# First expert block's gating before the fourth scored block, v split in two around the gating, decay chain first in the mixer

## The chip, the cores and the metric

The kernel runs on one core of a Trainium2 chip. The metric is the device time of one execution in microseconds. TensorE (PE) multiplies and loads its weights on a second track (PEld), VectorE (DVE) and ScalarE (ACT) work element by element, GpSimd (POOL) gathers rows and starts some transfers, SyncE (SP) starts most transfers.

## The reference

One decoder layer over 512 tokens of width 1024, all in float32: an adaLN-modulated norm, one input projection that feeds a gated MLP and a gated delta rule with a short causal convolution, an output projection, then a retrieval layer over 128 x 128 = 16,384 single-neuron experts and a last norm. What matters here:

```python
q, k, v = silu(short_conv(p[q, k, v columns], conv_w))          # 4 taps along the tokens
g = -exp(a_log) * softplus(a + dt_bias); beta = sigmoid(b)        # decay of the delta rule
# retrieval: each token has 8 heads x 16 experts (ids) with softmax gates
act = gelu(einsum('pd,phkd->phk', hb, expert_u[ib]))
out = einsum('phk,phkd->pd', gb * act, expert_v[ib])
```

## The kernel before

Float32 products are made of three matmuls (lines 78 to 80): each operand is split into a high part, rounded by a copy (ACT as a rule), and a low part, the difference (`split_lo`, line 83, DVE as a rule); the products high x high, low x high and high x low are added up. So each block of weights needs an ACT copy and, after it, a DVE subtraction before its second matmul.

The stages, by the trace: modulation sums and first norm (0 to 53 us), the mixer (53 to about 340), output projection and the second norm, queries and top-16 routing (to 575), the gates written out dense and 47 of the 128 expert blocks scored early (to 733), the expert stage (733 to 1590), the end (to 1624).

**Mixer.** PE's order is written by hand: `ORD` lists projections (`k2`, `q3`), lengths (`l0` to `l3`, the squared norms of k and q by head), `d` (the decay matrices) and `f` (filling matmuls of v). Where the other engines' instructions stand is decided by a scheduler, by priorities; `tc.high_priority(n)` moves what is written inside it ahead by n places in that ranking. `conv_silu` (line 189) makes one 128 x 512 tile of the convolution: ACT copies the projection `pp` from PSUM to `xp` (line 195), DVE multiplies it by the first tap (196) and adds three shifted ones (198), ACT applies silu (199). The decay chain (lines 361 to 375) is some 20 tiny DVE operations on 128 x 16 with one exponential on ACT; it ends in `g`, and `beta` is a sigmoid. `pg` (line 420) is the first matmul that needs `g`; `pks` (385) are the transposes of k and q; `py` (524) are matmuls of the triangular solve, whose input `ms` DVE makes. Behind it DVE also makes modulation sums that are needed later (`wada`, line 208).

**Expert stage.** All engines run in the order of the program here. Three tiles of 128 tokens are dense (TD = 384): for each block of 128 experts the scores `pS` are 24 matmuls of 128x384 (lines 829 to 849), for the 81 blocks that were not scored early; the values `acc` are 18 matmuls of 128x512. The fourth tile of tokens goes by rows gathered for each of 128 picks: two DVE operations each (lines 1077, 1087). In `before(n)` and after it, iteration n makes what later iterations need:

- `split_v(n + 1)`: copy `vhi` on ACT (1137), difference `vlo` on DVE.
- `load_v(n + 3)`, `load_a(n + 3)`: transfers on SP; for an early block `sgr`, its stored scores; for every eighth block also the gates of eight blocks (1.5 MB, line 1116).
- the picks that are due, then `gated(n + 2)`: `a` = scores x gates on DVE (1122), its copy `ahi` on ACT (1124), `alo` on DVE.
- PE: values of block n, then scores of block n + 4, for which `split_u` has made `uhi` (ACT, 829) and `ulo` (DVE).

Before the loop, four blocks are scored (line 1202), then `split_v(0)` and `gated(0)`, `gated(1)` stand. The values of the last three blocks (125 to 127) are computed tile by tile, and `finish(t)` (line 1153) applies the last norm to each of the three dense tiles: line 1175 is its last multiplication by halves.

Of the kernel before, what the change touches and what calls it, by code (L numbers as in the profile page):

```python
# [59 lines left out]
def layer(ctx: ExitStack, tc: tile.TileContext, I, out):  # L60
# [88 lines left out]
    with ExitStack() as mixer:  # L149
# [42 lines left out]
        def conv_silu(c, dst, tmp, w=None, place=stream):  # L192
            def done(pp):
                xp, acc = tmp(), tmp()
                nc.scalar.copy(xp, pp)
                nc.vector.tensor_scalar(acc, xp, convw[:, c, 3:4], None, op0=OP.mult)
                for j in range(1, 4):
                    nc.vector.scalar_tensor_tensor(acc[:, j:], xp[:, :S - j], convw[:, c, 3 - j:4 - j], acc[:, j:], op0=OP.mult, op1=OP.add)
                nc.scalar.activation(dst, acc, AF.Silu)

            return project(w or I["w_in_t"][c], *hs, done, place)
# [111 lines left out]
        with ExitStack() as gdn, tc.manual_schedule(engines={nc.tensor.engine}):  # L313
# [47 lines left out]
            nc.vector.tensor_tensor(ga, ab[:, :, 0:H], bc(dtb[:, None, :], [P, NT, H]), op=OP.add)  # L361
            nc.vector.scalar_tensor_tensor(e, ga, -1.0, ga, op0=OP.mult, op1=OP.max)
            nc.scalar.activation(e, e, AF.Exp, scale=-1.0)
            nc.vector.tensor_scalar(s1, e, 2.0, None, op0=OP.add)
            nc.vector.reciprocal(s1, s1)
            nc.vector.tensor_tensor(s1, s1, e, op=OP.mult)
            nc.vector.tensor_tensor(s2, s1, s1, op=OP.mult)
            nc.vector.tensor_scalar(po, s2, 2.0 / 17, 2.0 / 15, op0=OP.mult, op1=OP.add)
            for q in (13, 11, 9, 7, 5, 3, 1):
                nc.vector.tensor_tensor(po, po, s2, op=OP.mult)  # L370
                nc.vector.tensor_scalar(po, po, 2.0 / q, None, op0=OP.add)
            nc.vector.tensor_tensor(po, po, s1, op=OP.mult)
            nc.vector.scalar_tensor_tensor(ga, ga, 0.0, po, op0=OP.max, op1=OP.add)
            g, beta, nbe = gcol("g"), gcol("beta"), gcol("nbe")
            nc.vector.tensor_tensor(g, ga, bc(nega[:, None, :], [P, NT, H]), op=OP.mult)
            nc.scalar.activation(beta, ab[:, :, H:2 * H], AF.Sigmoid)
# [678 lines left out]
    with ExitStack() as experts, tc.manual_schedule():  # L1055
# [48 lines left out]
        def load_a(b, place=None):  # L1104
            if kinds[b]:
                sgl = place or ap_.tile([P, TD], F32, tag="sgr", name="sgr", bufs=3)
                nc.sync.dma_start(sgl, sgd[early.index(b)])
                ready["s", b] = sgl
# [8 lines left out]
        def gated(b):  # L1117
# [6 lines left out]
            nc.scalar.copy(ahi, a)  # L1124
            alo = ap_.tile([P, TD], F32R, tag="alo", name="alo", bufs=LAST + 1)
# [8 lines left out]
        def split_v(b):  # L1134
            raw = ready.pop(("v", b))
            hi = vp.tile([P, D], F32R, tag="vhi", name="vhi", bufs=LAST)
            nc.scalar.copy(hi, raw)  # L1137
            lo = vp.tile([P, D], F32R, tag="vlo", name="vlo", bufs=LAST)
            split_lo(nc.vector, lo, raw, hi)
            ready["vs", b] = hi, lo  # L1140
# [12 lines left out]
        def finish(t, ff, eng):  # L1153
# [17 lines left out]
            for i, cs in enumerate(halves):  # L1171
                if i:
                    nc.scalar.mul(x2[:, cs], y[:, cs], rs[:, 0:1])
                else:
                    nc.vector.tensor_scalar(x2[:, cs], y[:, cs], rs[:, 0:1], None, op0=OP.mult)
# [12 lines left out]
        for i in range(3):  # L1188
            load_a(i)
# [12 lines left out]
        for b in range(LEAD):  # L1202
            score_ahead(b, b < LEAD - 1)
        split_v(0)
        for b in range(2):
            gated(b)
# [4 lines left out]
        def before(n):  # L1211

            if n + 1 < NK:
                split_v(n + 1)
            if n + 3 < NK and n + 3 not in aside:
                load_v(n + 3)
                load_a(n + 3)

        picked_tile = finish(NDT, [facc[:, :512], facc[:, 512:]], nc.gpsimd)
        for n in range(NK - LAST):  # L1220
# [14 lines left out]
            gated(n + 2)  # L1235
# [7 lines left out]
        for n in range(NK - LAST, NK - 1):  # L1243
            before(n)
            if n + 2 < NK:
                gated(n + 2)
# [53 lines left out]
```

## Time and profile before

| | us |
|---|---|
| median of 3 runs | 1622.62 (1621.18 to 1624.57) |
| the profiled execution | 1626.11 |
| its span, first to last instruction | 1624.4 |
| PE / PEld / DVE / ACT / POOL busy | 1551.5 / 1370.3 / 1298.5 / 637.4 / 479.9 |
| mean granted clock of PE | 0.981 of full speed |

The profile is of one execution. A matmul's shown duration overlaps the next one's, so that the distance between two starts is what it costs; in the timelines the bracket behind a row is the idle time of that engine just before it and what ended it.

### The profile page before, as it was taken

The numbers are of one execution on the slowest core, as the hardware profiler recorded it, in microseconds if no ns is written. First come the engines' busy times: TensorE is split into PE (matmuls) and PEld (weight loads), VectorE is DVE, ScalarE is ACT, GpSimd is POOL, SyncE is SP. The second block draws the span as 40 slices with busy tenths as digits, with TensorE's granted clock in tenths as the row PEclk, the third lists the DMA queues.
The fourth block names the chain that finished last, engine by engine and source line by source line (L and its number), as shares of the span: only waits on it lengthen the run. The fifth ranks groups of instructions, "written<-read, shape, count | busy, mean of one in ns | idle before, by whom it ended". The sixth has DMA issues, their size and how long they took to land.

```text
span 1624.4 us, 22848 instructions
## 1 busy us (share of the span) xinstructions
PE 1551.5 (96%) x8499; PEld 1370.3 (84%) x8499; DVE 1298.5 (80%) x2470; ACT 637.4 (39%) x939; POOL 479.9 (30%) x362
## 2 busy tenths in 40 slices
PE   6889999999998989999999999999999999999996
PEld 5678988887897979998888888888888888888884
DVE  6999845556999999974688888887888888888766
ACT  4542224344345545653333333333333333333334
POOL 0000000005436600001244444444444454544210
PEclk9989999999999999999999999999999999999998
DMA  9343511354214567777899999999899999999872
GB/s 373 123 162 103 188 53 56 107 173 133 79 59 128 164 229 290 280 268 251 299 329 342 347 360 314 341 355 335 312 350 368 347 320 338 340 339 322 301 243 98
DMA packets 135086, 402.80 MB, mean 248 GB/s; under 512 B 12480, under 2 KB 50752, under 8 KB 133312
## 3 DMA queue, kind: packets, MB, share of 16 engines
q1 hardware_dynamic: 96800, 262.41, 46.5%
q0 software_dynamic: 38176, 138.95, 23.2%
q8 instruction: 66, 1.08, 0.3%
q14 instruction: 44, 0.36, 0.1%
HBM read 362.71 MB, written 38.60 MB: 247 GB/s over the span
## 4 chain that ended last, share of the span: by engine, by line
PE 67%; DVE 17%; DMA 6%; issue 5%; ACT 4%; SPq 0%; POOL 0%; DVEq 0%; ACTq 0%
PE pS L78 8%; PE acc L78 8%; PE acc L79 8%; PE acc L80 8%; PE pS L80 8%; PE pS L79 7%; DMA uraw<-in_u_t 3%; PE pp L78 3%; PE pp L79 3%; PE pp L80 3%; DMA wada<-in_w_ada_c 2%; PE pq L79 2%; PE pq L80 2%; PE pq L78 2%; DVE wada L208 2%
## 5 line engine op out<-in xcount | busy, mean ns | idle before, releaser
L1070 POOL DMA_INDIRECT u_rows<-in_u_rows,rows x128 | 205.2, 1603 | 554.2 <-DVE dots L1077 338.0
L78 PE MATMUL pS<-hhi,uhi 128*128 128x384 f32 x1024 | 354.7, 346 | 1.4 <-ACT uhi L829 1.4
L80 PE MATMUL pS<-hhi,ulo 128*128 128x384 f32 x1024 | 347.0, 339 | 9.4 <-POOL ulo L83 7.5
L79 PE MATMUL pS<-hlo,uhi 128*128 128x384 f32 x1024 | 345.6, 337 | 0.0
L78 PE MATMUL acc<-vhi,ahi 128*128 128x512 f32 x768 | 302.7, 394 | 6.3 <-ACT ahi L1124 3.8
L79 PE MATMUL acc<-vlo,ahi 128*128 128x512 f32 x768 | 301.6, 393 | 2.3 <-DVE vlo L83 2.3
L80 PE MATMUL acc<-vhi,alo 128*128 128x512 f32 x768 | 300.8, 392 | 0.0
L1124 ACT CAST ahi<-a 128x384 fp32r<-128x384 f32 x128 | 65.7, 513 | 480.6 <-DVE a L1122 480.6
L80 PEld LDWEIGHTS pS<-hhi,ulo 128*128 128x128 f32 x1024 | 193.9, 189 | 12.2 <-POOL ulo L83 8.8
L78 PEld LDWEIGHTS pS<-hhi,uhi 128*128 128x128 f32 x1024 | 194.0, 189 | 5.4 <-ACT uhi L829 2.5
L83 DVE TENSOR_TENSOR vlo<-vraw,vhi 128x1024 fp32r<-128x1024 f32 x126 | 154.4, 1225 | 54.0 <-ACT vhi L1137 47.1
L79 PEld LDWEIGHTS pS<-hlo,uhi 128*128 128x128 f32 x1024 | 194.2, 190 | 2.8
L78 PEld LDWEIGHTS acc<-vhi,ahi 128*128 128x128 f32 x768 | 145.0, 189 | 34.9 <-ACT ahi L1124 4.2
L79 PEld LDWEIGHTS acc<-vlo,ahi 128*128 128x128 f32 x768 | 145.2, 189 | 34.5 <-DVE vlo L83 6.9
L1070 POOL DMA_INDIRECT v_rows<-in_v_rows,rows x128 | 150.7, 1177 | 76.7 <-DVE facc L1087 37.4
L80 PEld LDWEIGHTS acc<-vhi,alo 128*128 128x128 f32 x768 | 145.1, 189 | 31.7
L83 DVE TENSOR_TENSOR ulo<-uraw,uhi 128x1024 fp32r<-128x1024 f32 x105 | 128.4, 1223 | 48.3 <-ACT uhi L829 48.3
L1087 DVE SCALAR_TENSOR_TENSOR facc<-v_rows,dots,facc 128x1024 f32<-128x1024 f32 x128 | 164.6, 1286 | 0.7
L1077 DVE CUSTOM_DVE_ANT_0 junk<-u_rows,h2tok 128x1024 bf16<-128x1024 f32 x128 | 155.9, 1218 | 0.1
L829 ACT CAST uhi<-uraw 128x1024 fp32r<-128x1024 f32 x128 | 133.7, 1048 | 38.4 <-PE pS L79 35.8
L1137 ACT CAST vhi<-vraw 128x1024 fp32r<-128x1024 f32 x126 | 131.3, 1042 | 0.0
L83 DVE TENSOR_TENSOR alo<-a,ahi 128x384 fp32r<-128x384 f32 x128 | 71.5, 559 | 74.2 <-ACT ahi L1124 74.2
(358 smaller groups left out, 2417.9 us busy)
## 6 DMA issues: line engine op xcount, KB each, us to landing
uraw<-in_u_t SPq DMA_DIRECT2D x128, 512.0 KB, 6.1
vraw<-in_v_rows SPq DMA_DIRECT2D x123, 512.0 KB, 5.4
gd<-scs SPq DMA_DIRECT2D x12, 2048.0 KB, 6.7
gates<-gd SPq DMA_DIRECT2D x15, 1536.0 KB, 13.3
wada<-in_w_ada_c SPq DMA_DIRECT2D x44, 512.0 KB, 4.3
raw<-in_w_in_t SPq DMA_DIRECT2D x24, 512.0 KB, 3.5
sgd<-sgl SPq DMA_DIRECT2D x47, 192.0 KB, 3.8
sgr<-sgd SPq DMA_DIRECT2D x45, 192.0 KB, 5.4
```

Of the source, the lines that this page charges most:

```text
L78: mm(o, ahi, bhi, start=start, stop=False)
L79: mm(o, ahi, blo, start=False, stop=False)
L80: mm(o, alo, bhi, start=False, stop=stop)
L83: eng.tensor_tensor(lo, full, hi.bitcast(F32), op=OP.subtract)
L208: nc.vector.tensor_tensor_reduce(w, w, scB, scale=1.0, scalar=0.0 if bias is None else bias[:, c:c + 1], op0=OP.mult, op1=OP.add, accum_ou ...
L829: nc.scalar.copy(hi, raw)
L1070: nc.gpsimd.indirect_dma_start(out=r, out_offset=None, in_=I[src], in_offset=bass.IndirectOffsetOnAxis(ap=rows_[:, j:j + 1], axis=0))
L1077: nc.vector.tensor_tensor_reduce(junk, rowsin.pop(("u_rows", j)), h2tok, scale=1.0, scalar=0.0, op0=OP.mult, op1=OP.add, accum_out=dots[j ...
L1087: nc.vector.scalar_tensor_tensor(facc, rowsin.pop(("v_rows", j)), d[:, j % GP:j % GP + 1], facc, op0=OP.mult, op1=OP.add)
L1124: nc.scalar.copy(ahi, a)
L1137: nc.scalar.copy(hi, raw)
```

## The change

Six edits, none to what is computed.

- In `conv_silu` the first tap is multiplied on ACT, from PSUM, instead of on DVE from the copy (12 tiles).
- The decay chain and `beta` stand in `tc.high_priority(QPR)`, QPR = 120.
- `split_v` is two functions, `split_v_hi` and `split_v_lo`; `gated(b, between)` calls `between` after it has issued `ahi` and before `alo`. `gated(n + 2)` moves into `before(n)`, ahead of the picks, with `split_v_lo(n + 1)` between its two parts.
- `load_a` is issued one iteration earlier, for block n + 4, and `sgr` has four buffers instead of three.
- Ahead of the loop three blocks are scored, then block 0 is gated and its v split, then the fourth block is scored.
- In `finish`, for the first two tiles, both halves of the last multiplication are on ACT.

```diff
--- before.py
+++ after.py
@@ -193,7 +193,7 @@
             def done(pp):
                 xp, acc = tmp(), tmp()
                 nc.scalar.copy(xp, pp)
-                nc.vector.tensor_scalar(acc, xp, convw[:, c, 3:4], None, op0=OP.mult)
+                nc.scalar.mul(acc, pp, convw[:, c, 3:4])
                 for j in range(1, 4):
                     nc.vector.scalar_tensor_tensor(acc[:, j:], xp[:, :S - j], convw[:, c, 3 - j:4 - j], acc[:, j:], op0=OP.mult, op1=OP.add)
                 nc.scalar.activation(dst, acc, AF.Silu)
@@ -358,22 +358,23 @@
             nc.scalar.copy(ab.rearrange("p a b -> p (a b)"), pab[:, :NT * 8])
 
             ga, e, s1, s2, po = gcol("ga"), gcol("e"), gcol("s1"), gcol("s2"), gcol("po")
-            nc.vector.tensor_tensor(ga, ab[:, :, 0:H], bc(dtb[:, None, :], [P, NT, H]), op=OP.add)
-            nc.vector.scalar_tensor_tensor(e, ga, -1.0, ga, op0=OP.mult, op1=OP.max)
-            nc.scalar.activation(e, e, AF.Exp, scale=-1.0)
-            nc.vector.tensor_scalar(s1, e, 2.0, None, op0=OP.add)
-            nc.vector.reciprocal(s1, s1)
-            nc.vector.tensor_tensor(s1, s1, e, op=OP.mult)
-            nc.vector.tensor_tensor(s2, s1, s1, op=OP.mult)
-            nc.vector.tensor_scalar(po, s2, 2.0 / 17, 2.0 / 15, op0=OP.mult, op1=OP.add)
-            for q in (13, 11, 9, 7, 5, 3, 1):
-                nc.vector.tensor_tensor(po, po, s2, op=OP.mult)
-                nc.vector.tensor_scalar(po, po, 2.0 / q, None, op0=OP.add)
-            nc.vector.tensor_tensor(po, po, s1, op=OP.mult)
-            nc.vector.scalar_tensor_tensor(ga, ga, 0.0, po, op0=OP.max, op1=OP.add)
             g, beta, nbe = gcol("g"), gcol("beta"), gcol("nbe")
-            nc.vector.tensor_tensor(g, ga, bc(nega[:, None, :], [P, NT, H]), op=OP.mult)
-            nc.scalar.activation(beta, ab[:, :, H:2 * H], AF.Sigmoid)
+            with tc.high_priority(QPR):
+                nc.vector.tensor_tensor(ga, ab[:, :, 0:H], bc(dtb[:, None, :], [P, NT, H]), op=OP.add)
+                nc.vector.scalar_tensor_tensor(e, ga, -1.0, ga, op0=OP.mult, op1=OP.max)
+                nc.scalar.activation(e, e, AF.Exp, scale=-1.0)
+                nc.vector.tensor_scalar(s1, e, 2.0, None, op0=OP.add)
+                nc.vector.reciprocal(s1, s1)
+                nc.vector.tensor_tensor(s1, s1, e, op=OP.mult)
+                nc.vector.tensor_tensor(s2, s1, s1, op=OP.mult)
+                nc.vector.tensor_scalar(po, s2, 2.0 / 17, 2.0 / 15, op0=OP.mult, op1=OP.add)
+                for q in (13, 11, 9, 7, 5, 3, 1):
+                    nc.vector.tensor_tensor(po, po, s2, op=OP.mult)
+                    nc.vector.tensor_scalar(po, po, 2.0 / q, None, op0=OP.add)
+                nc.vector.tensor_tensor(po, po, s1, op=OP.mult)
+                nc.vector.scalar_tensor_tensor(ga, ga, 0.0, po, op0=OP.max, op1=OP.add)
+                nc.vector.tensor_tensor(g, ga, bc(nega[:, None, :], [P, NT, H]), op=OP.mult)
+                nc.scalar.activation(beta, ab[:, :, H:2 * H], AF.Sigmoid)
 
 
             ssq = gcol("ssq", (P, 2, NT, H))
@@ -1103,7 +1104,7 @@
 
         def load_a(b, place=None):
             if kinds[b]:
-                sgl = place or ap_.tile([P, TD], F32, tag="sgr", name="sgr", bufs=3)
+                sgl = place or ap_.tile([P, TD], F32, tag="sgr", name="sgr", bufs=4)
                 nc.sync.dma_start(sgl, sgd[early.index(b)])
                 ready["s", b] = sgl
             if b % GB == 0:
@@ -1114,7 +1115,7 @@
                 if b:
                     nc.sync.dma_start(groups[b // GB], gview[:, :, b:b + GB])
 
-        def gated(b):
+        def gated(b, between=None):
 
             sgl = ready.pop(("s", b)) if kinds[b] else scored.pop(b)
             a = ap_.tile([P, TD], F32, tag="a", name="a")
@@ -1122,6 +1123,8 @@
             nc.vector.tensor_tensor(chunked(a), chunked(sgl), groups[b // GB][:, :, b % GB], op=OP.mult)
             ahi = ap_.tile([P, TD], F32R, tag="ahi", name="ahi", bufs=LAST + 1)
             nc.scalar.copy(ahi, a)
+            if between:
+                between()
             alo = ap_.tile([P, TD], F32R, tag="alo", name="alo", bufs=LAST + 1)
             split_lo(nc.vector, alo, a, ahi)
             ready["a", b] = ahi, alo
@@ -1131,10 +1134,13 @@
             eng.dma_start(raw, I["v_rows"][b * NK:(b + 1) * NK])
             ready["v", b] = raw
 
-        def split_v(b):
-            raw = ready.pop(("v", b))
+        def split_v_hi(b):
             hi = vp.tile([P, D], F32R, tag="vhi", name="vhi", bufs=LAST)
-            nc.scalar.copy(hi, raw)
+            nc.scalar.copy(hi, ready["v", b])
+            ready["vhi", b] = hi
+
+        def split_v_lo(b):
+            raw, hi = ready.pop(("v", b)), ready.pop(("vhi", b))
             lo = vp.tile([P, D], F32R, tag="vlo", name="vlo", bufs=LAST)
             split_lo(nc.vector, lo, raw, hi)
             ready["vs", b] = hi, lo
@@ -1169,7 +1175,7 @@
             nc.vector.tensor_tensor(rs, ss[:, 0:1], ss[:, 1:2], op=OP.add)
             inverse_rms(rs, rs, D)
             for i, cs in enumerate(halves):
-                if i:
+                if i or t < NDT - 1:
                     nc.scalar.mul(x2[:, cs], y[:, cs], rs[:, 0:1])
                 else:
                     nc.vector.tensor_scalar(x2[:, cs], y[:, cs], rs[:, 0:1], None, op0=OP.mult)
@@ -1185,7 +1191,7 @@
         load_u(new[2])
         load_u(new[3])
         split_u(new[1], nc.vector)
-        for i in range(3):
+        for i in range(4):
             load_a(i)
 
         def score_ahead(b, split=True):
@@ -1199,11 +1205,13 @@
                 advance(expert_scores(b))
                 nnew += 1
 
-        for b in range(LEAD):
-            score_ahead(b, b < LEAD - 1)
-        split_v(0)
-        for b in range(2):
-            gated(b)
+        for b in range(LEAD - 1):
+            score_ahead(b, True)
+
+        split_v_hi(0)
+        gated(0, lambda: split_v_lo(0))
+        score_ahead(LEAD - 1, False)
+        gated(1)
         split_u(new[LEAD], nc.vector)
 
         aside = (NK - 2, NK - 1)
@@ -1211,10 +1219,15 @@
         def before(n):
 
             if n + 1 < NK:
-                split_v(n + 1)
+                split_v_hi(n + 1)
+            if n + 2 < NK:
+                gated(n + 2, lambda: split_v_lo(n + 1))
+            elif n + 1 < NK:
+                split_v_lo(n + 1)
             if n + 3 < NK and n + 3 not in aside:
                 load_v(n + 3)
-                load_a(n + 3)
+            if n + 4 < NK and n + 4 not in aside:
+                load_a(n + 4)
 
         picked_tile = finish(NDT, [facc[:, :512], facc[:, 512:]], nc.gpsimd)
         for n in range(NK - LAST):
@@ -1232,7 +1245,6 @@
                     load_a(b, sp.tile([P, TD], F32, tag="sgl", name="slast"))
             if n >= NK - LAST - SPARE:
                 advance(picked_tile, 1)
-            gated(n + 2)
             expert_values(n, n == 0)
             score_ahead(n + LEAD)
         advance(picks)
@@ -1242,8 +1254,6 @@
             advance(steps, 1)
         for n in range(NK - LAST, NK - 1):
             before(n)
-            if n + 2 < NK:
-                gated(n + 2)
         for t in range(NDT):
             for i in range(2):
                 for n in range(NK - LAST, NK):
```

Where the instructions then stand. PE's and POOL's order is the same in both kernels; on DVE, ACT and SP only the mixer, the expert stage and the end differ.

DVE in the steady part of the expert stage, one iteration with a new block and one pick, before (`ulo`, `vlo`, `alo` are low parts; `junk` and `facc` are a pick):

```order
L83 TENSOR_TENSOR ulo<-uraw,uhi 128x1024
L83 TENSOR_TENSOR vlo<-vraw,vhi 128x1024
L1077 ISA junk,dots<-u_rows,h2tok 128x1024
L1077 ISA dots 128x1
L1087 SCALAR_TENSOR_TENSOR facc<-v_rows,dots,facc 128x1024
L1122 TENSOR_TENSOR a<-sgl,gates 128x384
L83 TENSOR_TENSOR alo<-a,ahi 128x384
```

The same iteration after:

```order
L83 TENSOR_TENSOR ulo<-uraw,uhi 128x1024
L1123 TENSOR_TENSOR a<-sgl,gates 128x384
L83 TENSOR_TENSOR vlo<-vraw,vhi 128x1024
L83 TENSOR_TENSOR alo<-a,ahi 128x384
L1078 ISA junk,dots<-u_rows,h2tok 128x1024
L1078 ISA dots 128x1
L1088 SCALAR_TENSOR_TENSOR facc<-v_rows,dots,facc 128x1024
```

`vlo` moved behind `a`, so that `a` and `alo` no longer stand next to each other, and the pick moved behind all three.

ACT at the start of the expert stage, before (`sgl` is the gelu that ends the scoring of a block; the first two rows are of the third and the fourth block):

```order
L849 ACTIVATE sgl<-pS 128x384
L849 ACTIVATE sgl<-pS 128x384
L1137 CAST vhi<-vraw 128x1024
L1124 CAST ahi<-a 128x384
L1124 CAST ahi<-a 128x384
```

And after (again from the third block on):

```order
L850 ACTIVATE sgl<-pS 128x384
L1139 CAST vhi<-vraw 128x1024
L1125 CAST ahi<-a 128x384
L850 ACTIVATE sgl<-pS 128x384
L1125 CAST ahi<-a 128x384
```

The high parts of v and of the first gated block moved ahead of the fourth block's `sgl`. On DVE the order there becomes `a`, `vlo`, `alo` from `vlo`, `a`, `alo`.

ACT in the mixer behind `ab`, the input of the decay chain, before (`whi` is the high part of a block of weights):

```order
L358 COPY ab<-pabt 128x32
L376 ACT_TABLE_LOAD
L376 ACTIVATE beta<-ab 128x16
L199 ACT_TABLE_LOAD
L199 ACTIVATE kT<-tmp 128x512
L199 ACTIVATE qT<-tmp 128x512
L195 COPY tmp<-pp 128x512
```

And after:

```order
L129 CAST whi<-raw 128x1024
L358 COPY ab<-pabt 128x32
L129 CAST whi<-raw 128x1024
L377 ACT_TABLE_LOAD
L377 ACTIVATE beta<-ab 128x16
L365 ACT_TABLE_LOAD
L365 ACTIVATE e<-e 128x16
L199 ACT_TABLE_LOAD
L199 ACTIVATE kT<-tmp 128x512
```

The chain's exponential `e` (line 365) now stands ahead of the first `kT`, with the table load that it needs, and two `whi` stand near it. On DVE the chain's rows stand earlier, and five `wada` products stand between the last norm and `g` where three stood.

## Rows read from the trace of the kernel before

**Rows 1.** windows of time: span, busy time of each engine, granted clock, DMA share, GB/s
```profile
53.00:85.00 32.00, 23.62 (x108) 18.45 (x107) 30.69 (x82) 21.04 (x30) 0.00 (x0) 0.91 0.56 178
752.00:758.00 6.00, 4.59 (x11) 3.63 (x12) 4.46 (x7) 2.92 (x4) 0.00 (x0) 0.50 0.49 179
1000.00:1100.00 100.00, 100.00 (x492) 88.79 (x491) 84.34 (x109) 34.39 (x50) 50.56 (x34) 1.00 0.95 344
```

**Rows 2.** waits of PE from 700 us on: total us, times, longest
```profile
PE acc L78 <- ACT ahi L1124: 3.8, 1, 3.8
PE acc L78 <- ACT vhi L1137: 2.5, 2, 1.2
PE acc L79 <- DVE vlo L83: 2.3, 4, 0.8
PE pS L80 <- DVE ulo L83: 1.9, 4, 0.6
```

**Rows 3.** waits of DVE over the whole run
```profile
DVE alo L83 <- ACT ahi L1124: 74.2, 128, 0.6
...
DVE vlo L83 <- ACT vhi L1137: 47.9, 62, 7.1
...
DVE a L1122 <- DMA gates<-gd: 4.6, 4, 2.3
```

**Rows 4.** timeline of PE, start of the expert stage: start, duration, instruction, [idle before <-releaser]
```profile
749.24 0.34 PE L80 MATMUL pS<-hhi,ulo 128*128 128x384 f32 x1
753.41 0.79 PE L78 MATMUL acc<-vhi,ahi 128*128 128x512 f32 x1 [3.83 <-ACT ahi L1124]
...
754.43 0.63 PE L80 MATMUL acc<-vhi,alo 128*128 128x512 f32 x1
754.85 0.63 PE L78 MATMUL acc<-vhi,ahi 128*128 128x512 f32 x1
```

**Rows 5.** timeline of ACT, start of the expert stage
```profile
745.50 0.49 ACT L849 ACTIVATE sgl<-pS 128x384 f32<-128x384 f32 x1 [2.73 <-issue]
...
750.05 1.04 ACT L1137 CAST vhi<-vraw 128x1024 fp32r<-128x1024 f32 x1
```

**Rows 6.** timeline of DVE, start of the expert stage
```profile
751.12 1.23 DVE L83 TENSOR_TENSOR vlo<-vraw,vhi 128x1024 fp32r<-128x1024 f32 x1 [7.09 <-ACT vhi L1137]
```

**Rows 7.** the two loads of the first gates (line 1112), issue to landing
```profile
L1112 SPq DMA_DIRECT2D gates<-gd x2: 377/956/1535, 740.4 to 740.8; - x2
...
DMA to landing us min/median/max: 7.9/9.0/10.1
```

**Rows 8.** the page's DMA issues, the other gates loads: count, KB each, median us
```profile
gates<-gd SPq DMA_DIRECT2D x15, 1536.0 KB, 13.3
```

**Rows 9.** timeline of PE, last phase
```profile
1595.13 0.39 PE L78 MATMUL acc<-vhi,ahi 128*128 128x512 f32 x1
```

**Rows 10.** timeline of DVE, last phase
```profile
1603.16 0.69 DVE L1163 TENSOR_TENSOR y<-acc,gt 128x512 f32<-128x512 f32 x1 [1.31 <-PE acc L80]
...
1606.09 0.69 DVE L1163 TENSOR_TENSOR y<-acc,gt 128x512 f32<-128x512 f32 x1 [0.78 <-PE acc L80]
```

**Rows 11.** waits of PE in the mixer, 54 to 160 us
```profile
PE pg L420 <- DVE g L375: 7.6, 1, 7.6
PE py L524 <- DVE ms L517: 3.9, 1, 3.9
PE pks L385 <- ACT qT L199: 3.7, 1, 3.7
PE pks L385 <- ACT kT L199: 0.8, 1, 0.8
```

**Rows 12.** timeline of ACT in the mixer
```profile
55.96 0.59 ACT L195 COPY tmp<-pp 128x512 f32<-128x512 f32 x1
```

**Rows 13.** timeline of DVE in the mixer
```profile
55.81 0.48 DVE L196 TENSOR_SCALAR tmp<-tmp,cols 128x512 f32<-128x512 f32 x1
...
82.41 0.17 DVE L375 TENSOR_TENSOR g<-ga,nega 128x16 f32<-128x16 f32 x1
```

## The prediction

> **What bounds the kernel now.** I read the windows first [rows 1]: in the steady part of the expert stage, at 1000 to 1100 us, PE is busy 100.00 of 100 us and DVE 84.34, while in the mixer, at 53 to 85 us, PE is busy only 23.62 of 32 us and DVE 30.69. So PE sets the time of the long stage and DVE that of the start of the mixer. Then the waits, because only those that PE sees count. From 700 us on PE waits for four things only [rows 2]: the first `ahi` 3.8 us, `vhi` 2.5, `vlo` 2.3, `ulo` 1.9, 10.5 us in all. DVE waits far more [rows 3]: 74.2 us for `ahi` in 128 pieces, 0.58 each, and 47.9 us for `vhi`. The first are forced by the order: `alo` stands right behind `a` and its operand goes through ACT in between. That sum is no forecast. DVE had this time to lose, since PE did not wait for it in the middle of the stage. Last I read the timelines at the two ends of the stage and in the mixer, where PE does stand still.
>
> **The start of the expert stage.** The last scoring matmul starts at 749.24, the first values matmul at 753.41 [rows 4]: 4.0 us later than the next one would have. `vhi(0)` starts at 750.05, behind the gelu of the fourth block [rows 5], `vlo(0)` at 751.12 [rows 6], and the gating only after it. After that gap PE runs slowly: starts at 754.43 and 754.85 are 0.42 us apart [rows 4], and the granted clock between 752 and 758 is 0.50 [rows 1], its 1.2 GHz level. At full clock 0.42 would be near 0.23 (the level is half and the distance nearly doubles), so twelve such matmuls cost some 2.4 us. Together 6.4 us.
> After the change this work stands ahead of the fourth block's gelu, beside the fourth block's scoring, which takes PE from the third gelu's start at 745.50 [rows 5] to 749.4, about 4 us. What starts it is then the later of that gelu's end (746) and the first half of the gates. The two loads are issued at 740.4 and 740.8 and land 7.9 and 10.1 us later [rows 7], so the first, which `a(0)` waits for, is there at 748.3 if the shorter time is its own, and at 750.5 if the longer is. I take 748.3, since it was issued first on the same queue. `a` (an estimate of 0.55, as it is of the same 128 x 384 as its copy), then 0.58 until that copy `ahi` is there [rows 3]: 749.4, when PE asks for it. `vlo(0)`, 1.23 long [rows 6], lies beside `ahi` and ends at 750.0, `alo` at 750.5, so PE loses about 0.8 in two small waits instead of 4.0, and I expect no slow clock behind so short a gap. Gain 6.4 - 0.8 = 5.6, less a little for `alo`: **5.5 us**. With the gates at 750.5 everything is 2.2 us later, most of the slow clock may stay, and the gain is 0.9; the other end is 6.4.
>
> **The steady part.** Per iteration DVE loses the 0.58 in front of `alo` (`vlo`, 1.23, covers it) and, since `vhi` is asked for earlier on ACT, its wait of up to 0.4 as well. That is some 120 us of DVE idle time, and next to nothing of it is PE's. The waits of PE that are not at the two ends are `ulo` 1.9 and about 0.5 of the `vlo` [rows 2]: **2.4 us**, all of which I count, because DVE gets ahead by far more. Lower end 0 (`ulo` now stands behind the picks, though still an iteration ahead of its use), upper end 5, twice the waits shown, because a wait also delays the weight load behind it.
> What is late next: `vlo(n + 1)` now stands behind `a(n + 2)`, and so behind the gates when a new group begins (a rival below). `load_a` is issued one iteration earlier, past nothing but `load_v` on SP; its 192 KB are small beside the 512 KB blocks on the same queue, and the fourth `sgr` buffer lets it start. I price it at nothing, and at the gates' lateness below if that is wrong.
>
> **The end.** The last phase begins with PE at 1595.13 [rows 9], and DVE takes its first result at 1603.16 [rows 10], 8.0 us for nine matmuls that need about 2.1. In between stand two rounds of `vhi` 1.2 and `vlo` 0.8 that PE waits for (4.0 of the 4.8 in [rows 2]), and slow matmuls behind them. DVE does `a`, wait, `alo`, wait, `vlo` for each of the last blocks, about 3.2 us a round. After the change a round is without both waits, some 2.2, and `gated(127)` is done a block earlier, so only block 127's v remains: its `vhi` needs the buffer that block 124 frees when the phase begins, then 1.04 [rows 5] and 1.23 [rows 6], about 1597.5, two more matmuls, first result at about 1598.1 on the old time scale: 5.0 earlier. The wait of 0.78 in front of the second result [rows 10] goes too, because at full clock PE makes a result in 2.1 us and DVE takes 2.2 for one (three operations of 0.69 and their gaps). From there DVE is back to back to the end and is the bound, so the two multiplications that move to ACT count in full: 0.48 each, by the same operation and shape in the mixer [rows 13], less a tenth at each where neighbours overlap, 0.8. Sum 5.0 + 0.8 + 0.8 = **6.6 us**, ends 3 (only one of the two rounds of waits goes) and 8.
>
> **The mixer.** PE's four waits up to 160 us are 7.6 for `g`, 3.9 for `ms`, 3.7 for the last `qT`, 0.8 for the first `kT` [rows 11]. DVE is the bound there, so I placed the instructions of the new order one after the other, each at the later of its engine and its inputs, with the durations of the old trace. The 12 first taps leave DVE, 12 x 0.48 [rows 13] less the overlap, about 4.8 us, and cost ACT 12 x 0.59 by the copy of the same tile [rows 12]: 7 us on an engine that is busy 21.04 of 32 us [rows 1]. `g` comes at about 79.7 instead of 82.41 [rows 13], not more, because two more `wada` products now stand ahead of it. But the first decay matrices come only 1.1 earlier, and `kT` comes some 2.5 later, behind the sigmoid, the exponential and a table load each: PE's wait for it goes from 0.8 to 3.3, inside the time in which it waited for `g` anyway. The last `qT` comes about 3.5 earlier, so that its wait shrinks from 3.7 to about 1.3, and the matmuls behind it are not at the low clock; the last `ms` comes about 5.4 earlier. That last number is the gain, and since the placing leaves out what transfers do, I take **4.5 us**, with -3 (rival below) and 7 as ends.
> The Trainium skill speaks against this edit: "ScalarE: Activation LUTs", "Rules for kernel authors", gives a plain multiplication to VectorE and not to ScalarE, and its section on table loads adds about 93 ns for a per-partition operand. By that the 12 taps would cost ACT about 8 us, an estimate from that page, more than DVE saves. The sum above goes by who is free, in this stretch ACT; by the page alone the edit would lose, which is part of the second rival's mechanism. No row shows a tap on ACT.
>
> **Sum.** 5.5 + 2.4 + 6.6 + 4.5 = 19.0 us off an execution of 1626.1, which is 3.5 above the median of 1622.6. I take the terms off the median, since all are differences: **1603.6 us**. The stages between mixer and expert stage keep their order on every engine and only move earlier.
>
> **The rivals.**
> *Late gates at the start, and no gain in the mixer.* The first half lands with the longer time, as two loads on one queue may share it; the mixer's freed DVE time is eaten by the longer ACT chain. Gain 0.9 + 2.4 + 6.6 + 0 = 9.9: about 1613. For it: the landing times are 2.2 apart and I don't know which is whose. Against: PE did wait 7.6 for `g`.
> *The mixer gets slower by 3.* `kT` behind two more table loads and `whi`, and `wada` products that wait for their transfers in front of `g`, so that the wait for `g` grows. 5.5 + 2.4 + 6.6 - 3 = 11.5: about 1611.
> *Slower: late gates now hold v.* Fifteen more groups take a median of 13.3 us to land [rows 8]; two iterations are about 13 on average, and 8.2 where two early blocks follow each other. Before, DVE waited for gates only four times, 4.6 us in all [rows 3], and what stood behind was one `alo`; now `vlo(n + 1)` stands behind, which PE needs one iteration later. It decides where the wait exceeds the slack of about 1.3 us of an iteration with an early block. If each of the 15 then cost 1.5 us and clock, the 19 would be gone: about 1626. Against it: the loads are issued an iteration earlier, and the waits seen are at most 2.3.
> *DVE was the real limit.* PE's 100.00 is of matmuls that overlap; its weight loads are busy 88.79 of 100 [rows 1]. If PE had that much room, 11 of 100 over 800 us, the 120 us that DVE wins would give up to 90: about 1530. The Trainium skill's "Perfetto Trace Analysis" says that matmul busy time is a poor measure of how near PE is to its limit and weight-load time a good one. Against it: PE's waits in the stage are a few us, and a PE that is held shows waits.
> *It does nothing that counts*, each freed wait being replaced by the next: about 1621.
>
> **Chances.** Forecast 0.63, late gates at the start 0.13, slower mixer 0.11, gates holding v 0.05, DVE the limit 0.02, nothing 0.06. Within 0.2% (3.2 us, about what this kernel's times can tell from no change) is the last, slower the gates; faster is the rest, 0.89. The range goes from 1595 (all upper ends but one) to 1615 (the two smaller gains); the forecast's own is 1598 to 1609.
>
> **What would show it.** At the start the gap between the last `pS` and the first `acc` about 1 us and no window at 0.50 there; DVE's waits for `ahi` nearly gone while PE stays at 100 in the middle; DVE's first result of the last phase about 3 us after the phase begins, instead of 8; in the mixer `g` some 3 us earlier and shorter waits for `qT`. It is wrong if PE shows new waits for `vlo` at every eighth block, if the wait for `g` does not shrink, or if the slow clock stays at the start.

## The result

The changed kernel takes 1599.14 us, the median of 4 runs (1598.25 to 1602.01), against 1623.59 for the kernel before on the same occasion (1621.18 to 1630.05): a ratio of 0.9846, 95% interval 0.9821 to 0.9871, or 24.5 us less (21 to 29). The forecast was 1603.6, 19.0 less.

The profiled execution took 1598.25 us. Its windows, in the columns of [rows 1]; 742 to 748 is the first values work, which was at 752 to 758:

```profile
53.00:85.00 32.00, 25.96 (x110) 20.30 (x109) 29.16 (x77) 22.26 (x34) 0.00 (x0) 0.89 0.63 208
742.00:748.00 6.00, 6.00 (x33) 5.53 (x32) 4.78 (x8) 3.47 (x4) 0.00 (x0) 1.00 0.53 193
1000.00:1100.00 100.00, 100.00 (x493) 89.04 (x492) 80.57 (x106) 35.86 (x52) 48.44 (x32) 1.00 0.94 339
```

In the middle PE is at 100.00 of 100 us, as before, with DVE at 80.57 instead of 84.34; the window holds another stretch of the same work now, with 106 DVE instructions instead of 109. At the start of the stage the granted clock is 1.00 where it was 0.50. In the mixer PE is busy 25.96 of 32 us instead of 23.62, but with 110 matmuls instead of 108: at 85 us it is only two matmuls ahead, and most of the mixer's gain comes later.

PE's waits over the whole run, those that answer to [rows 2] and [rows 11]:

```profile
PE pks L386 <- ACT kT L199: 3.2, 1, 3.2
PE py L525 <- DVE ms L518: 3.1, 1, 3.1
PE pd L413 <- DVE X L410: 2.8, 1, 2.8
...
PE pks L386 <- ACT qT L199: 1.0, 1, 1.0
...
PE acc L79 <- DVE vlo L83: 0.8, 1, 0.8
```

From the start of the expert stage on one wait of 0.8 is left of 10.5 us. DVE's waits, for [rows 3]:

```profile
DVE vlo L83 <- ACT vhi L1139: 160.6, 70, 5.0
...
DVE ulo L83 <- ACT uhi L830: 19.2, 6, 9.8
...
DVE a L1123 <- DMA gates<-gd: 5.4, 2, 4.3
...
DVE alo L83 <- ACT ahi L1125: 0.6, 1, 0.6
```

And one line of before that [rows 3] leaves out:

```profile
DVE ulo L83 <- ACT uhi L829: 48.3, 80, 9.8
```

The 74.2 us in front of `alo` have shrunk to 0.6, and yet DVE waits no less than before: the waits for `ahi`, `vhi` and `uhi` add up to 170.4 us before and to 180.4 now. They have moved to a place where they cost nothing. DVE is ahead, and waits for `vhi`, which ACT makes behind a gelu that waits for PE. In the middle of the stage this reads, on ACT and then on DVE:

```profile
1021.24 0.49 ACT L850 ACTIVATE sgl<-pS 128x384 f32<-128x384 f32 x1 [2.79 <-PE pS L80]
1021.63 1.04 ACT L1139 CAST vhi<-vraw 128x1024 fp32r<-128x1024 f32 x1
```

```profile
1022.70 1.23 DVE L83 TENSOR_TENSOR vlo<-vraw,vhi 128x1024 fp32r<-128x1024 f32 x1 [2.53 <-ACT vhi L1139]
1023.85 0.55 DVE L83 TENSOR_TENSOR alo<-a,ahi 128x384 fp32r<-128x384 f32 x1
```

So DVE is held by PE, which is the engine that bounds.

The marks of the two profiled executions, from the starts of the named instructions (the last scoring matmul of all is that of line 78), show where the time went:

| mark | before | after | gain so far |
|---|---|---|---|
| last `py` from X and `ms`, end of the solve | 184.6 | 177.9 | 6.7 |
| first `pqs` on the delta rule's state | 235.6 | 226.3 | 9.3 |
| last scoring matmul ahead of the stage | 749.24 | 739.34 | 9.9 |
| first values matmul | 753.4 | 739.7 | 13.7 |
| last scoring matmul of all | 1569.5 | 1548.8 | 20.7 |
| last DVE instruction | 1619.9 | 1592.1 | 27.8 |

### The profile page after: what moved, and what is told of

Read it like the earlier page. It is cut to its first block, busy times and chain, and to the rows that moved or that the text cites. A ratio compares the mean times of both kernels' runs of the same rounds, so it can differ in the third digit from the quotient of the medians.

```text
span 1596.5 us, 22855 instructions
## 1 busy us (share of the span) xinstructions
PE 1540.2 (96%) x8499; PEld 1365.8 (86%) x8499; DVE 1270.7 (80%) x2456; ACT 646.2 (40%) x954; POOL 493.8 (31%) x362
## 4 chain that ended last, share of the span: by engine, by line
PE 86%; DVE 8%; DMA 2%; ACT 2%; issue 1%; POOL 1%; SPq 0%; ACTq 0%; DVEq 0%; POOLq 0%
PE acc L78 11%; PE acc L80 11%; PE acc L79 11%; PE pS L78 11%; PE pS L80 10%; PE pS L79 10%; PE pp L79 3%; PE pp L78 3%; PE pp L80 3%; DMA wada<-in_w_ada_c 2%; PE pq L79 2%; PE pq L80 2%; PE pq L78 2%; PE pgb L1014 1%; PE pgb L1015 1%
## 5 line engine op out<-in xcount | busy, mean ns | idle before, releaser
L1071 POOL DMA_INDIRECT u_rows<-in_u_rows,rows x128 | 211.6, 1653 | 530.1 <-DVE dots L1078 320.2
L850 ACT ACTIVATE sgl<-pS 128x384 f32<-128x384 f32 x128 | 62.8, 490 | 320.9 <-PE pS L80 310.8
L1071 POOL DMA_INDIRECT v_rows<-in_v_rows,rows x128 | 157.4, 1230 | 76.9 <-DVE facc L1088 38.0
```

The lines of the kernel that those rows point to most:

```text
L850: nc.scalar.activation(sgl, pS[:, :TD], AF.Gelu_apprx_tanh)
L1071: nc.gpsimd.indirect_dma_start(out=r, out_offset=None, in_=I[src], in_offset=bass.IndirectOffsetOnAxis(ap=rows_[:, j:j + 1], axis=0))
```

## The experiments

Each was run against the kernel before on the same chip; a gain is the ratio of the medians times the 1624.5 to 1625.1 us of before in that session.

| run | ratio, 95% interval | us against before |
|---|---|---|
| both mixer edits | 0.9967, 0.9953 to 0.9981 | -5.4 |
| tap on ACT alone | 0.9941, 0.9922 to 0.9960 | -9.6 |
| chain priority alone | 0.9972, 0.9949 to 0.9994 | -4.5 |
| expert stage and end alone | 0.9892, 0.9868 to 0.9916 | -17.5 |
| start alone | 0.9982, 0.9968 to 0.9997 | -2.9 |
| steady order and loads alone | 0.9917, 0.9903 to 0.9932 | -13.5 |
| last multiplications alone | 0.9996, 0.9982 to 1.0011 | -0.7 |
| changed, loads as before | 1.0001, 0.9988 to 1.0014 | +0.2 |
| before, DVE work added | 1.0037, 1.0020 to 1.0054 | +6.0 |
| changed, DVE work added | 0.9859, 0.9839 to 0.9879 | -22.9 |
| changed, gates alone early | 0.9851, 0.9830 to 0.9871 | -24.2 |
| changed, no chain priority | 0.9840, 0.9818 to 0.9863 | -26.0 |

**Both mixer edits.** The kernel before with the first two edits of the diff (line 196 and the `high_priority` block).

> Only the two edits of the mixer (first tap on ACT, decay chain with high priority). The trace of the changed kernel begins the queries' scoring 9.6 to 10 us earlier than before. If the whole of that is the mixer's order: about 9.5 us faster. If part of it is only where PE's low clock happened to fall behind the solve (about 3 us of it), then 5.5 to 7 us faster. If the mixer's gain needs the expert stage's edits: no difference.

Measured 5.4 us faster (3.1 to 7.6): nearest to the second case. In its trace the solve ends at 177.7, 6.9 earlier, as in the changed kernel, but `pqs` starts only at 230.8. Between the two marks stands the same program on PE in all these kernels, and it takes 48.4 us in the changed kernel, 51.0 in the kernel before, 53.1 here, 54.6 with the tap alone and 48.5 with the last multiplications alone. The windows of 200 to 216 us show why, here of the kernel before, the tap alone, and the last multiplications alone, one line each:

```profile
200.00:216.00 16.00, 16.00 (x102) 13.88 (x101) 4.48 (x7) 3.81 (x7) 0.00 (x0) 0.79 0.21 67
```

```profile
200.00:216.00 16.00, 16.00 (x80) 13.45 (x79) 4.59 (x7) 1.18 (x2) 0.00 (x0) 0.57 0.20 66
```

```profile
200.00:216.00 16.00, 16.00 (x133) 14.43 (x132) 6.40 (x10) 4.07 (x8) 0.00 (x0) 1.00 0.22 78
```

PE is busy in all 16 us each time, with 102, 80 and 133 matmuls at a granted clock of 0.79, 0.57 and 1.00. A stretch at the 1.2 GHz level falls there in some executions and not in others, whatever was edited; at 0.57 it is some 14 of the 16 us, worked out from the two levels. What sets it off is open. Over the whole distance of 46.9 to 55.3 us in all the traces PE is idle for 2.0 us at most, so the clock makes the difference.
The mark ahead of it moves too, though less. In the six traces whose mixer is that of before the solve ends between 182.8 and 184.9, in the five with both edits between 177.7 and 180.1. The means, 183.9 and 178.7, are 5.2 apart, close to the 5.4 of the times. So of the 9.9 us of the profile's mark some 5 belong to the mixer's order, and most of the rest to where the low clock fell.

**Tap alone, chain alone.** One edit each:

```diff
-                nc.vector.tensor_scalar(acc, xp, convw[:, c, 3:4], None, op0=OP.mult)
+                nc.scalar.mul(acc, pp, convw[:, c, 3:4])
```

> Only the first tap of the convolution on ACT. If DVE's 12 x 0.4 us in front of the solve are what counts: about 4.5 us faster. If a multiplication on ACT costs more than it saves on DVE (the rule of the rival theory, ACT busy some 7 us more): no difference or up to 3 us slower. If both edits are needed together: under 2 us.

> Only the decay chain and beta with high priority, taps on DVE. If the earlier g is what counts: 2 to 5 us faster. If kT, which comes later behind the sigmoid and the exponential with their table loads, takes it back: no difference or up to 3 us slower.

The tap gives 9.6 (6.5 to 12.7), more than any theory said, the chain 4.5 (1.0 to 8.3). Both together gave no more than the tap alone, with intervals that overlap. By the mark at the end of the solve, which the later stretch does not touch, the tap alone gains 8.1 (176.5), the chain alone 5.5 (179.1), both 6.9 (177.7), each in one execution of a mark that moves by about 2; the mixer with the tap alone ends its solve at 178.5 in `no_chain`. The profiled execution with the tap alone took 1627.34, far above its median of 1615.24: its stretch behind the solve took 54.6 and its expert stage 820.5 where before had 51.0 and 816.1. PE's waits in the mixer, first with the tap alone, then with the chain alone:

```profile
PE pg L420 <- DVE g L375: 5.9, 1, 5.9
PE py L524 <- DVE ms L517: 3.1, 1, 3.1
PE pks L385 <- ACT qT L199: 1.0, 1, 1.0
```

```profile
PE pks L386 <- ACT kT L199: 2.3, 1, 2.3
PE pd L413 <- DVE X L410: 2.0, 1, 2.0
```

The tap takes the waits for `g`, `qT` and `ms` down. The chain's priority removes the wait for `g`, and puts a longer one for `kT` (2.3) and one for `X` (2.0) in its place. `g` came earlier, and what PE did next waited in part for something else. All waits of PE between 54 and 182 us add up to 16.0 us before, 12.5 with the chain alone, 11.5 with the tap alone, 13.3 with both.

**No chain priority.** The changed kernel with that block taken back.

> The changed kernel without the high priority of the decay chain. By the mark at the end of the triangular solve (last py at 176.5 with the tap alone, 177.9 in the changed kernel): 1 us faster than the changed kernel, not to be told from it by the times. If chain and tap add up (the sum of the two alone, 14 us by the times): 4 to 5 us slower than the changed kernel.

Ratio 0.9840 (0.9818 to 0.9863), median 1599.02: the same as the changed kernel. The two edits do not add up, and once the tap is moved no gain of the chain's priority is left that the times show; PE's waits in the mixer add up to 11.1 us here and to 11.7 in the changed kernel. This is as fast as the changed kernel with one edit fewer, and no run was faster beyond the noise.

**Expert stage and end alone.** All but the mixer's edits.

> Only the edits of the expert stage and the end. By the marks of the two traces: start 5.6, steady part 5.2, end 7.2, sum 18 us faster. If the parts are not independent (the stage gains only because it begins at another time against the transfers): clearly less, 10 to 14.

17.5 us faster (13.6 to 21.4). With the 5.4 of the mixer that makes 22.9 of 24.5, the same within the noise. The marks say more sharply that the halves are independent: the stage from its first values matmul to the last scoring takes 809.1 us here, in the changed kernel and in `no_chain`, and the end behind it 43.3 in all three.

**Start alone.** The kernel before with the new stage start; in the loop `split_v` keeps its two parts together. The last part of its edit:

```diff
-        for b in range(LEAD):
-            score_ahead(b, b < LEAD - 1)
-        split_v(0)
-        for b in range(2):
-            gated(b)
+        for b in range(LEAD - 1):
+            score_ahead(b, True)
+        split_v_hi(0)
+        gated(0, lambda: split_v_lo(0))
+        score_ahead(LEAD - 1, False)
+        gated(1)
```

> Only the order at the start of the expert stage (first gating and v's two parts ahead of the fourth scored block), all else as before. Theory: PE's gap of 4.0 us and the twelve matmuls at the low clock go, 5 to 6 us faster. Rival: the gates' landing decides and the low clock stays, about 1 us faster. Second rival: DVE, which has no time to spare in the stage, gives it back later, 2 to 3 us faster.

The times say 2.9 (0.5 to 5.2), less than the 5 to 6 that theory said and what the second rival said. The trace has the theory's picture. No wait for `ahi` is left, and the first values work runs at full clock, where [rows 1] has 0.50 for the same window:

```profile
752.00:758.00 6.00, 6.00 (x28) 5.02 (x29) 4.25 (x6) 2.52 (x3) 0.00 (x0) 1.00 0.68 260
```

28 matmuls in 6 us against 11. From the first early scoring to the last scoring of all the trace is 5.3 us shorter than before (1101.0 against 1106.3). The waits for `ulo` stay, 2.2 us in all. From the last scoring to the last DVE instruction it takes 51.4 instead of 50.4, which could be the rival's loss. Whether the rest of the difference is the noise of the 1.2 GHz stretches or a loss elsewhere is open: the interval's end is just there.

**Steady order and loads alone.** The expert edits without the new start and without the last multiplications.

> Only the new order inside an iteration, with the loads one block earlier and four sgr buffers; the start scores all four blocks first as before, the last multiplications stand where they stood. Theory: the steady part gives 5 and the end about 6.5 (all of it but the two multiplications), 11 to 12 us faster, and the start keeps its gap of 4 us with the low clock. Rival: freed DVE time gives nothing in the steady part, so only the end, 6 us.

13.5 (10.9 to 15.8). By its marks the stage from its first values matmul to the last scoring takes 810.9 instead of 816.1 us, and from there to the last DVE instruction 44.4 instead of 50.4: 11.2, as the theory had it. Freed DVE time does count in the steady part, 5.2 us of it.

**Last multiplications alone.** The kernel before with `if i or t < NDT - 1:` in `finish`.

> Only the two last multiplications moved from DVE to ACT. Theory: DVE is back to back there, 0.8 us faster, too small to be told from no change by the times; in the trace the distance from the first y to the last row on DVE falls from 16.8 to about 16 us. Rival: ACT's answer comes later than DVE's and the wait of 0.78 for PE swallows it, no change in that distance.

0.7 us by the times, not to be told from nothing. On DVE, from the second `y` of the phase to its last row; the first line is of before, and belongs to 1606.09 in [rows 10]:

```profile
1619.93 0.49 DVE L1175 TENSOR_SCALAR x<-y,rsf 128x512 f32<-128x512 f32 x1
```

```profile
1604.46 0.69 DVE L1163 TENSOR_TENSOR y<-acc,gt 128x512 f32<-128x512 f32 x1 [1.70 <-PE acc L80]
...
1617.25 0.49 DVE L1175 TENSOR_SCALAR x<-y,rsf 128x512 f32<-128x512 f32 x1
```

That is 12.8 us against 13.8: the theory's 1.0 is there. From the first `y` on it is 16.6 against 16.8, because PE, at a granted clock of 0.55 between 1600 and 1606 where the trace of before has 0.72, makes the second result later (a wait of 1.70 instead of 0.78). That hid most of the gain in this execution; it is not the rival, since the wait ends ahead of the multiplications that were moved. In the kernel with all expert edits the distance from the first `y` is 14.9, without this edit 15.9 (`steady_alone`'s marks 1592.8 and 1608.7), 1.0 again.

**Changed, loads as before.** `load_a(n + 3)` and three `sgr` buffers again.

> The changed kernel, with the loads of gates and stored scores again three blocks ahead instead of four, and three sgr buffers. If the fourth block of lead is what keeps late gates from holding v: DVE waits for the gates of each group, PE waits for vlo at many of the 15 groups, 5 to 20 us slower than the changed kernel. If the lead is not needed: the same time within 2 us, with DVE waits for gates of a few us in all.

The whole gain is gone: 1.0001 (0.9988 to 1.0014), 25 us slower than the changed kernel, more than the 5 to 20 that I expected. DVE's waits for gates in the expert stage, then PE's waits:

```profile
DVE a L1123 <- DMA gates<-gd: 76.6, 14, 10.2
```

```profile
PE acc L79 <- DVE vlo L83: 15.1, 8, 4.0
PE acc L78 <- ACT vhi L1139: 1.1, 1, 1.1
```

One of the 14 late groups on DVE:

```profile
1406.84 0.56 DVE L1123 TENSOR_TENSOR a<-sgl,gates 128x384 f32<-128x384 f32 x1 [7.91 <-DMA gates<-gd]
1407.32 1.22 DVE L83 TENSOR_TENSOR vlo<-vraw,vhi 128x1024 fp32r<-128x1024 f32 x1
```

`a` waits 7.91 us for the gates, `vlo` of the next block stands right behind it, and PE stands 3.85 us from 1404.7 until `vlo` is there, then runs at a granted clock of 0.57 from 1408 to 1412. Sixteen us of PE's waits and the slow matmuls behind three of them make the stage 833.6 us long instead of 809.1. In the kernel before it takes 816.1: without the lead the new order is worse than the old one. The lead alone, in the old order, was not run.

**Gates alone early.** The changed kernel, with the gates in a function of their own that is called four blocks ahead. The last part of its edit:

```diff
             if n + 3 < NK and n + 3 not in aside:
                 load_v(n + 3)
-            if n + 4 < NK and n + 4 not in aside:
-                load_a(n + 4)
+                load_a(n + 3)
+            if n + 4 < NK:
+                load_gates(n + 4)
```

> The changed kernel with only the gates loaded four blocks ahead; the stored scores again three ahead, with three buffers. If the gates' landing is the whole of what the earlier loads are for: within 2 us of the changed kernel (about 1600). If the stored scores, which the later of two queued blocks can hold up, count as well: DVE waits for sgr, 2 to 8 us slower than the changed kernel.

0.9851, median 1601.45: the same as the changed kernel, and its stage takes the same 809.1 us. DVE's waits for transfers are few, the longest for gates ahead of the loop:

```profile
DVE a L1125 <- DMA sgr<-sgd: 5.7, 3, 3.8
DVE a L1125 <- DMA gates<-gd: 4.6, 2, 4.4
```

So in the stage it is the gates' 1.5 MB whose lead matters, not the stored scores and not the fourth buffer. At the end the stored scores may count a little: the 3.8 us in front of `a` fall at 1573.6, and the end takes 45.5 us instead of 43.3, too little for the times to tell.

**DVE work added, before and changed.** Each block's `split_lo(nc.vector, alo, a, ahi)` stands twice.

> The kernel before, with each block's alo subtraction done twice (the same result written again; 128 more DVE instructions of 0.45 to 0.56 us, some 60 us of DVE work in the expert stage). If DVE's forced waits had left it no time to spare: 30 to 60 us slower. If PE alone sets the stage and DVE has room: under 5 us.

> The changed kernel with the same 128 additional DVE instructions. If the change gave DVE time to spare, about 1.2 us per block by its busy share of 80.6 of 100 us: at most 3 us slower than the changed kernel (the end of the stage alone), and PE still 100 of 100 in the middle. If DVE is still at its limit: 30 us or more slower. If weight loads, not matmul starts, told PE's room, DVE's loss of 60 us would show in part.

Some 60 us of DVE work cost 6.0 us (3.3 to 8.8) before. On the changed kernel the ratio is 0.9859 against its 0.9846, some 2 us that the times don't tell from nothing. By the marks of one execution its stage takes 1.4 us longer (810.5) and its end 4.1 (47.4), somewhat more than the theory allowed, and PE is busy 99.45 of the 100 us, not 100. The run on the kernel before speaks against its own first theory, by which forced waits leave DVE nothing. DVE's waits between 735 and 1600 us, first before, then with the work added:

```profile
DVE vlo L83 <- ACT vhi L1137: 47.5, 61, 7.1
DVE ulo L83 <- ACT uhi L829: 44.6, 79, 9.8
```

```profile
DVE alo L83 <- ACT ahi L1124: 73.1, 126, 0.6
DVE vlo L83 <- ACT vhi L1138: 26.5, 14, 7.1
DVE ulo L83 <- ACT uhi L829: 13.9, 3, 9.8
```

The wait for `ahi` stays, 73.1, but those for `vhi` and `uhi` fall from 92.1 together to 40.4, while DVE's busy time in these 865 us grows from 692.1 to 746.2. The added instructions took 54 us, nearly all of it out of these waits. A forced wait behind an instruction is time that another instruction can use.

## Why the prediction was right, term by term

**Start, 5.5.** Right. In the changed kernel's trace PE and DVE read:

```profile
739.34 0.34 PE L80 MATMUL pS<-hhi,ulo 128*128 128x384 f32 x1
739.67 0.51 PE L78 MATMUL acc<-vhi,ahi 128*128 128x512 f32 x1
740.21 0.50 PE L79 MATMUL acc<-vlo,ahi 128*128 128x512 f32 x1
740.68 0.50 PE L80 MATMUL acc<-vhi,alo 128*128 128x512 f32 x1
```

```profile
738.46 0.56 DVE L1123 TENSOR_TENSOR a<-sgl,gates 128x384 f32<-128x384 f32 x1 [4.33 <-DMA gates<-gd]
738.94 1.22 DVE L83 TENSOR_TENSOR vlo<-vraw,vhi 128x1024 fp32r<-128x1024 f32 x1
```

The first values matmul stands 0.33 behind the last scoring one, 0.16 more than the 0.17 between two of those, and the next two distances are 0.54 and 0.47 instead of 0.23: with 0.1 at the fourth together the forecast 0.8, and no low clock. `a(0)` waited for the gates until 738.46, 8.0 us after the first load's issue at 730.5, so the shorter landing time was the first half's, as chosen. By the marks 13.7 - 9.9 = 3.8, and the first block's values take 1.7 less inside the stage, the low clock's 2.4 less the small losses: 5.5 in all. The bound of 0.9 did not come.

**Steady part, 2.4.** Too small: about 5.2, by the marks of the experiment with this edit alone. The step that was off is the price of PE's waits, which was taken from the idle rows of its matmuls. Those are five, 2.4 us in all; the waits of the second track, PEld, for the same operands add up to 7.4 in the same trace. Waits of PEld between 760 and 1570 us, before:

```profile
PEld acc L79 <- DVE vlo L83: 3.7, 13, 0.9
PEld pS L80 <- DVE ulo L83: 3.2, 4, 1.0
PEld pS L78 <- ACT uhi L829: 0.5, 2, 0.2
```

One of them, as PEld and as PE show it:

```profile
1163.58 0.19 PEld L80 LDWEIGHTS pS<-hhi,ulo 128*128 128x128 f32 x1 [0.96 <-DVE ulo L83]
```

```profile
1163.58 0.44 PE L80 MATMUL pS<-hhi,ulo 128*128 128x384 f32 x1 [0.65 <-DVE ulo L83]
```

This matmul starts 0.98 behind the one before instead of 0.17, and the next 0.28 behind it. What it costs is 0.9, of which PE's idle row shows 0.65: the shown duration of the matmul ahead covers a part, and the next start is late too. In the trace with this edit alone PEld has no such wait in that stretch, and the gain of 5.2 lies between the two sums. The upper end, twice the idle time, was the better value.

**End, 6.6.** Right: from the last scoring matmul of all to the last DVE instruction 50.4 became 43.3, 7.1 less. The phase begins with PE at 1573.80, the last block's `vlo` ends PE's last wait as forecast, and DVE takes its first result 3.4 us behind the start (3.0 forecast, 8.0 before) and is back to back from there:

```profile
1573.80 0.39 PE L78 MATMUL acc<-vhi,ahi 128*128 128x512 f32 x1
```

```profile
1575.12 1.23 DVE L83 TENSOR_TENSOR vlo<-vlast,vhi 128x1024 fp32r<-128x1024 f32 x1 [1.48 <-ACT vhi L1139]
1577.17 0.69 DVE L1169 TENSOR_TENSOR y<-acc,gt 128x512 f32<-128x512 f32 x1 [0.82 <-PE acc L80]
...
1579.25 0.69 DVE L1169 TENSOR_TENSOR y<-acc,gt 128x512 f32<-128x512 f32 x1
```

**Mixer, 4.5.** Right within the noise: 5.4 by the times, 5.2 by the mean marks at the end of the solve. The placing gave `g` at 79.7 instead of 82.41; it came at 80.53:

```profile
80.53 0.17 DVE L376 TENSOR_TENSOR g<-ga,nega 128x16 f32<-128x16 f32 x1
```

PE was busy with projections until 81.1 and did not wait for it. The placing gave a wait for `kT` of 3.3 (3.2), for `qT` of 1.3 (1.0), and a start of the work behind `ms` 5.4 earlier (`py` from X at 148.0 instead of 153.6, 5.6). That the last agrees so well is in part luck: this mark lies between 151.4 and 154.1 in the traces whose mixer is that of before, between 147.4 and 149.8 with both edits. It did not name the new waits, 2.8 for `X` and 1.2 for `krk`. ACT's price was too low, 7 us where the taps took 8.3. The gain was put down to both edits together; the runs show that each gains alone and that both give no more than the tap, since the chain's priority moves PE's wait from `g` to `kT` and `X`.
The Trainium skill's rule ("ScalarE: Activation LUTs", "Rules for kernel authors") would have kept the tap on VectorE. The price from its section "What ACT_TABLE_LOAD costs" is borne out: the tap on ACT, with its per-partition operand, takes 692 ns against 578 for the copy of the same tile, 114 more where the page has about 93 for such an operand.

```profile
L196 ACT ACTIVATE tmp<-pp,cols x12: 677/692/712, 56.1 to 139.3; 128x512 f32<-128x512 f32 x12
```

```profile
L195 ACT COPY tmp<-pp x12: 563/578/587, 55.6 to 138.8; 128x512 f32<-128x512 f32 x12
```

ACT pays 12 x 0.69 = 8.3 us for 12 x 0.48 = 5.8 us on DVE, and the kernel is faster, since DVE is the late engine in that stretch and ACT is not (busy 30.69 and 21.04 of 32 us in [rows 1]).

**The rivals.** Late gates holding `v` did not happen in the changed kernel, but the mechanism is real. With one block less of lead it costs 25 us, near the 22 that the rival was priced at (15 groups at 1.5); by PE's rows it is nine waits, three of them long. It was unlikely only for the lead, and the chance of 0.05 stood on an edit that the prediction priced at nothing: without that edit the whole gain is gone. That DVE was the real limit is refuted: PE stays at 100.00 of 100 with DVE's busy share at 80.57, and 60 us more of DVE work cost some 2, not to be told from nothing. The weight loads' 88.79 of 100 was no room either: the stage became 7.0 us shorter and not up to 90, and their share is 89.04 now. So the weight-load share of "Perfetto Trace Analysis" in the Trainium skill ("Identifying the Most-Contended Engine") does not by itself find the limit of this stage; the waits of PE and PEld do. The sum missed 5.5 us of 24.5; by the marks 2.8 are the steady part's, about 0.7 the mixer's and 0.5 the end's, and the rest is within the interval of 21 to 29. The range's lower end, 1595, is not what its words give: all four upper ends, 6.4 + 5 + 8 + 7 = 26.4, give 1596.2.

## What to carry to other kernels

Put the waits of the bounding engine in the sum, never those of an engine that has time, and read them on the weight-load track too, where each is longer than the matmul's idle row shows. When an instruction is put behind one that waits for a transfer, price the lead of that transfer before anything else: the order that made the stage 7.0 us shorter with one more block of lead made it 17.5 longer without it. An instruction moved to an engine on which it is slower can still be a gain where the other engine is late.

## What the runs showed of the hardware

One and the same sequence on PE, between the end of the solve and the delta rule's state, took from 46.9 us to 55.3 in executions of kernels that do not differ there, with granted clocks between 200 and 216 us from 0.57 to 1.00 and PE idle for 2.0 us at most. Differences of 3 to 5 us between single executions of this kernel are within that, and only marks on either side of such a stretch, or many runs, tell an edit of a few us from it.
